# A sample convolution as one product and sum per block, and norm gains applied from PSUM

## The chip, the cores and the metric

The kernel runs on one core of one Trainium2 chip. The metric is the device time of one launch in microseconds (us); lower is better. The time before is the median of three runs.

## What is computed

Two layers (DEPTH = 2) of a decoder for 512 prompt rows (one sequence) and 32 sample rows (8 sequences of 4 new tokens over a paged cache of 2048 positions). Each layer has a mixing part and a gated feed-forward part (FFN):

```python
def hybrid_layer(x, pos, conv_prev, pool_prev, attend, lam_init, p):
    z = rms_norm(x, p['g_mix_pre']) @ p['w_in']              # 1024 -> 2048
    a, ga, u, vb, q, k, v, xd = jnp.split(z, IN_SPLITS, axis=-1)
    ya, conv_new = conformer_conv(a, ga, conv_prev, ...)     # causal depthwise conv, 31 taps, 256 channels
    ...
    mix = jnp.concatenate([ya, yb, yc, yd], axis=-1) @ p['w_out']
    x = x + rms_norm(mix, p['g_mix_post'])
    gate, up = jnp.split(rms_norm(x, p['g_ffn_pre']) @ p['w_gu'], 2, axis=-1)
    x = x + rms_norm((jax.nn.silu(gate) * up) @ p['w_down'], p['g_ffn_post'])
```

The convolution of the sample rows takes 30 earlier rows of state and 4 new ones for each of the 8 sequences: for each of 256 channels (two blocks of 128, the index c) and 32 output tokens, 31 products and their sum. The two places with `rms_norm(...)` behind w_out and w_down are the transitions that the change touches.

## The kernel before, in words

**Numbers.** Weights arrive as fp32 tiles of 128x1024 (`raw`), are cast to a high part `whi` by ScalarE (L194) and a low part `wlo` by VectorE or GpSimd (L197); a product is three matmuls per contraction tile (L130). Activations carry the same two parts, `xhi` and `xlo`.

**Prompt rows.** For a layer the function `mixing` makes the w_in products and the four mixers. Then `prompt` runs `project_last` for w_out: eight (token tile of 128 rows, half of 512 columns) products of 24 matmuls, in the order of W_OUT_TURNS: (0,0) (1,0) (0,1) (1,1) (2,0) (2,1) (3,0) (3,1). Behind each product ScalarE copies the PSUM bank `acc` to `m` (L1282), squares `m` with a running sum (L1286), and GpSimd multiplies `m` by the norm's gain (L1287; VectorE in the last product). When both halves of a tile are there, `finish` makes the factor of the norm (L1297, then `rsqrt`, L177 on VectorE and L178 on GpSimd), the new residual `x_t` (L1305), its squares (L1310), the next norm's rows `m` (L1312), and `turn` (L239 to L242): TensorE transposes `m` into PSUM (`sx`), ScalarE casts that to `xhi`, VectorE subtracts to get `xlo`. Only then can FFN products use the tile. w_down's last chunk goes the same way at the end of the layer, with an add of the PSUM bank to `m` (L1284, VectorE) in place of the copy. At the very end of the kernel the residual of the last tile is made in two halves (L1302).

**Sample rows.** A background generator, `sample`, is interleaved with this. In the mixing part and the transition it runs `sample_pool`, `sample_gate` and `sample_conv`; the latter does the 31 taps by a chain of VectorE instructions of 128x32 (L883), with the buffers of tag "pr" (two of them) for what is loaded and stored (`sst`, `cn`). Behind the convolution come its layer norm, the queries, and the paged attention: per layer 32 gathers of keys (`kr`, L997) and 32 of values (`vr`, L1027) of 512 KB each, issued on GpSimd's queue, four and four for a sequence. Three `kr` and four `vr` buffers are in rotation: a value buffer is free again when TensorE has done the products `sx<-vr` with it.

**Order.** The order of every engine's instructions is fixed when the kernel is built, by a scheduler with its own model of durations; on the chip each engine runs its list in order, waiting on semaphores. So a change of some instructions moves others.

```python
        for t in range(1, CW):
            for c in range(2):
                V.scalar_tensor_tensor(a[:, c], ext[:, c, :, t:t + 4], pf[:, 8 + 2 * t + c:9 + 2 * t + c], a[:, c],
                                       op0=ALU.mult, op1=ALU.add)
...
            if first:
                S.copy(m[t][:, hs], o)
            else:
                V.tensor_tensor(m[t][:, hs], m[t][:, hs], o, op=ALU.add)
...
            (V if (t, half) == (3, 1) else G).tensor_tensor(m[t][:, hs], m[t][:, hs], gain[:, hs], op=ALU.mult)
```

Of the kernel before, what the change touches and what calls it, by code (L numbers as in the profile page):

```python
# [16 lines left out]
DM = 1024  # L17
# [15 lines left out]
# PSUM banks of the two halves of a layer, in address order  # L33
# [3 lines left out]
# priority of the gating chain; buffers of attention weights, and how far scores run ahead of them  # L37
# [3 lines left out]
# input-projection weights whose low part is taken on VectorE  # L41
NV = 1
# convolution taps that ScalarE and GpSimd take
NOFF = 8
# order of w_out's (token tile, half) products, and of its contraction tiles
W_OUT_TURNS = [(0, 0), (1, 0), (0, 1), (1, 1), (2, 0), (2, 1), (3, 0), (3, 1)]
W_OUT_ORDER = (6, 7, 0, 1, 2, 3, 4, 5)
# steps of the sample rows' flow per unit of the prompt's: in the transition, before and while they share weights
# [3 lines left out]
# first FFN feature tile whose weights the sample rows take from the prompt's tiles  # L52
F0 = 10
# buffers of the sample rows' flow; value tiles per round; how far scores run ahead of values
# [10 lines left out]
# columns of the constant block  # L65
C_ID, C_KG, C_BO, C_IW, C_IC, C_QS, C_END = 0, 128, 160, 162, 164, 196, 200
# columns of the sample-attention constant block
# [57 lines left out]
def trunk(ctx, tc, A, O):  # L125
# [18 lines left out]
    def ps():  # L144
        return psx("ps")
# [27 lines left out]
    def rsqrt(pool, src, P, n, scale, eps, tag):  # L173
        """(src * scale + eps) ** -0.5 on a [P, n] block."""
# [47 lines left out]
    def dense_fm(pair, c0, n, tag="acc"):  # L222
        """feature-major product of one weight tile with columns c0..c0+n of the tokens."""
# [9 lines left out]
    def turn(src, P, c0, tag="ps"):  # L233
        """token rows src, transposed into columns c0.. of xhi / xlo."""
# [9 lines left out]
    def finish_sample(fp, parts, m_s, x_t, stage, gpo, gpr, dst, tag):  # L244
        """the sample rows' sublayer output, still in four parts: x_t + its RMS norm, stored; then the RMS norm of that,
        transposed into dst, or xhi / xlo."""
# [90 lines left out]
    # =====================================================================  # L337
    # mixing sub-layer of the prompt (and the input projection of all tokens)
    # =====================================================================
# [12 lines left out]
    def mixing(l, mp, early):  # L352
# [57 lines left out]
        # -- A: convolution  # L410
# [61 lines left out]
        # -- C: attention  # L472
        ST = {}

        def stack():
            for c in range(2):
                st = ST[c] = {}
                # keys out
# [94 lines left out]
        # -- B: spatial gating  # L573
# [52 lines left out]
        # -- D: pooling  # L626
# [226 lines left out]
    def sample_conv(l, mp, cmn):  # L853
# [25 lines left out]
        for c in range(2):  # L879
            V.tensor_scalar(a[:, c], ext[:, c, :, 0:4], pf[:, 8 + c:9 + c], pf[:, c:c + 1], op0=ALU.mult, op1=ALU.add)  # L880
        for t in range(1, CW):
            for c in range(2):
                V.scalar_tensor_tensor(a[:, c], ext[:, c, :, t:t + 4], pf[:, 8 + 2 * t + c:9 + 2 * t + c], a[:, c],  # L883
                                       op0=ALU.mult, op1=ALU.add)
            if t % 4 == 0:
                yield
        o = ps()
# [14 lines left out]

    # =====================================================================
    # sample rows: paged attention, output projection and FFN
    # =====================================================================
    def sample(l, sp, share):
        ys = sp.tile([128, 8, NT], F32, tag="ys", name="ys")
        hs_in = sp.tile([128, 8, NT], F32, name="hs_in")
# [563 lines left out]
```

## Time and profile before

| | |
|---|---|
| time, median of 3 runs | 1460.94 us (1460.93 to 1461.8) |
| span of the profiled execution | 1463.0 us |
| TensorE matmul busy | 1376.9 us, 94% of the span |
| VectorE busy | 832.6 us, 57% |
| ScalarE busy | 499.5 us, 34% |
| GpSimd busy | 451.0 us, 31% |
| chain that ended last | TensorE 72%, VectorE 14%, DMA 5%, GpSimd 3% |

The span is that of one execution taken by the profiler, 2.06 us above the median of the timed runs. PE is TensorE, DVE VectorE, ACT ScalarE, POOL GpSimd, SP SyncE. A busy share is a mean over stages with different limits; the chain says which engine or transfer was waited for, step by step back from the end. The clock column of a table by stretches is the granted TensorE clock as a share of its full speed.

### The profile page before, as it was taken

Reading aid. Unit: us, or ns where it says so; the run is one execution under the profiler, and the core shown is the slowest. Engines: PE = TensorE matmul, PEld = TensorE weight load, DVE = VectorE, ACT = ScalarE, POOL = GpSimd, SP = SyncE. Lnnn points to the kernel's source line nnn. Section 1 sums busy time; section 2 is a strip of 40 time slices with the busy share of each in tenths; the row PEclk is TensorE's granted clock in tenths of the full one; section 3 lists DMA queues with packets and bytes.
Section 4 is the critical chain, followed back from the end, with each engine's and each line's share of the span. In section 5 each row is a group of like instructions: output and inputs, shape, how many; then the busy total and the mean of one; then the engine's idle time right before and its main releaser. Section 6 shows DMA issues by size and latency. Waiting matters only on the chain.

```text
span 1463.0 us, 22985 instructions
## 1 busy us (share of the span) xinstructions
PE 1376.9 (94%) x9114; PEld 1084.0 (74%) x9114; DVE 832.6 (57%) x1536; ACT 499.5 (34%) x987; POOL 451.0 (31%) x415
## 2 busy tenths in 40 slices
PE   6779997999999999999987799989999999999997
PEld 6768876877666777777777788878776667777775
DVE  4986779776434333433659767878664332333344
ACT  4326724332224321222343266333322332222231
POOL 4667545455300000000346685653543000000003
PEclk9989998999999999999998899999999999999999
DMA  6225234888858751233432252466887497213132
GB/s 199 87 69 159 90 120 145 282 317 291 289 169 254 236 180 64 67 107 105 162 105 73 78 149 87 160 217 226 340 302 246 155 309 231 97 58 115 58 133 90
DMA packets 160092, 242.15 MB, mean 166 GB/s; under 512 B 10444, under 2 KB 118226, under 8 KB 159986
## 3 DMA queue, kind: packets, MB, share of 16 engines
q1 hardware_dynamic: 141410, 173.32, 36.9%
q0 software_dynamic: 18432, 67.12, 12.4%
q8 instruction: 72, 1.18, 0.3%
q14 instruction: 34, 0.28, 0.1%
q10 hardware_dynamic: 144, 0.26, 0.0%
HBM read 222.33 MB, written 12.04 MB: 160 GB/s over the span
## 4 chain that ended last, share of the span: by engine, by line
PE 72%; DVE 14%; DMA 5%; issue 3%; POOL 3%; ACT 1%; SPq 0%; DVEq 0%; POOLq 0%; ACTq 0%
PE acc L130 55%; PE sx L130 10%; DVE cacc L422 6%; PE ps L130 3%; DVE sca L883 2%; DMA kr<-in_cache_k_dram,ik 2%; PE s L130 1%; POOL wlo L197 1%; DVE m L1312 1%; PE oT L130 1%; DVE wlo L197 1%; DMA raw<-in_w_in_dram 1%; DMA lq<-in_lambda_k_dram 1%; DVE x_t L1305 1%; PE ps L1012 0%
## 5 line engine op out<-in xcount | busy, mean ns | idle before, releaser
L130 PE MATMUL acc<-xhi,whi 128*128 128x512 f32 (+2 forms) x1152 | 411.6, 358 | 27.1 <-ACT qT L393 15.4
L130 PE MATMUL acc<-xlo,whi 128*128 128x512 f32 (+2 forms) x1152 | 409.0, 355 | 3.4 <-DVE xlo L242 3.4
L130 PE MATMUL acc<-xhi,wlo 128*128 128x512 f32 (+2 forms) x1152 | 409.9, 356 | 0.7 <-POOL wlo L197 0.6
L194 ACT CAST whi<-raw 128x1024 fp32r<-128x1024 f32 x178 | 184.1, 1048 | 298.2 <-PE acc L130 255.9
L130 PEld LDWEIGHTS acc<-xhi,whi 128*128 128x128 f32 x1152 | 223.7, 195 | 67.7 <-ACT qT L393 15.8
L197 DVE TENSOR_TENSOR wlo<-raw,whi 128x1024 fp32r<-128x1024 f32 x144 | 185.6, 1295 | 111.9 <-ACT whi L194 107.7
L130 PEld LDWEIGHTS acc<-xlo,whi 128*128 128x128 f32 x1152 | 224.0, 194 | 34.0 <-issue 4.1
L130 PEld LDWEIGHTS acc<-xhi,wlo 128*128 128x128 f32 x1152 | 224.0, 195 | 32.2 <-issue 4.9
L130 PE MATMUL acc<-whi,h 128*128 128x512 f32 x704 | 226.8, 397 | 0.0
L1287 POOL TENSOR_TENSOR m<-m,g_g_ffn_post 128x512 f32<-128x512 f32 x14 | 19.9, 1423 | 493.0 <-ACT junk L1286 493.0
L130 PEld LDWEIGHTS acc<-whi,h 128*128 128x128 f32 x704 | 131.1, 188 | 44.1 <-issue 11.1
L130 PE MATMUL acc<-wlo,h 128*128 128x512 f32 x352 | 138.6, 395 | 0.0
L422 DVE SCALAR_TENSOR_TENSOR cacc<-hext,pf,cacc 128x512 f32<-128x512 f32 x88 | 115.6, 1336 | 1.9
L197 POOL TENSOR_TENSOR wlo<-raw,whi 128x1024 fp32r<-128x1024 f32 x36 | 96.6, 2691 | 57.1 <-ACT whi L194 57.0
L997 POOL DMA_INDIRECT kr<-in_cache_k_dram,ik x64 | 73.9, 1155 | 106.7 <-DVE kt L1000 73.2
L178 POOL TENSOR_TENSOR rsw<-rsw,mhalf 128x1 f32<-128x1 f32 (+3 forms) x66 | 42.3, 645 | 184.9 <-DVE rsw L177 181.6
L1000 DVE STREAM_TRANSPOSE kt<-kr 128x1024 f32<-128x1024 f32 x64 | 78.3, 1232 | 28.2 <-DMA kr<-in_cache_k_dram,ik 18.5
L1027 POOL DMA_INDIRECT vr<-in_cache_v_dram,iv x64 | 62.8, 981 | 57.0 <-PE sx L130 40.3
L130 PEld LDWEIGHTS acc<-wlo,h 128*128 128x128 f32 x352 | 66.1, 188 | 17.6 <-issue 4.5
L1356 DVE SCALAR_TENSOR_TENSOR th<-th,acc 128x512 f32<-128x512 f32 (+1 forms) x46 | 29.7, 647 | 82.5 <-PE acc L130 82.2
L1165 DVE SCALAR_TENSOR_TENSOR sth<-sth,ps 128x64 f32<-128x64 f32 x22 | 4.8, 220 | 86.4 <-ACT sth L1164 86.4
L130 PE MATMUL sx<-vr,pt 128*32 128x256 f32 x512 | 49.8, 381 | 0.0
(405 smaller groups left out, 1939.6 us busy)
## 6 DMA issues: line engine op xcount, KB each, us to landing
raw<-in_w_gu_dram SPq DMA_DIRECT2D x44, 1024.0 KB
raw<-in_w_down_dram SPq DMA_DIRECT2D x20, 1024.0 KB
rws<-in_w_gu_dram SPq DMA_DIRECT2D x40, 512.0 KB
raw<-in_w_in_dram SPq DMA_DIRECT2D x16, 1024.0 KB
raw<-in_w_out_dram SPq DMA_DIRECT2D x8, 1024.0 KB
rwo<-in_w_out_dram SPq DMA_DIRECT2D x16, 512.0 KB
rws<-in_w_down_dram SPq DMA_DIRECT2D x16, 512.0 KB
x<-x_t SPq DMA_DIRECT2D x12, 512.0 KB
```

The source lines that it names most:

```text
L130: T.matmul(out, lhsT, rhs, start=start, stop=stop)
L178: G.tensor_tensor(y, v, mhalf[:P, :n], op=ALU.pow)
L194: S.copy(hi, src)
L197: eng.tensor_tensor(lo, src, hi.bitcast(F32), op=ALU.subtract)
L422: V.scalar_tensor_tensor(a, hext[c][:, t:t + SEQ], pf[:, 8 + 2 * t + c:9 + 2 * t + c], a, op0=ALU.mult, op1=ALU.add)
L883: V.scalar_tensor_tensor(a[:, c], ext[:, c, :, t:t + 4], pf[:, 8 + 2 * t + c:9 + 2 * t + c], a[:, c], op0=ALU.mult, op1=ALU.add)
L997: G.indirect_dma_start(out=kr, out_offset=None, in_=ck, in_offset=bass.IndirectOffsetOnAxis(ap=ik[:, s, bg:bg + 1], axis=0))
L1000: V.transpose(kt, kr)
L1027: G.indirect_dma_start(out=v.rearrange("p t e -> p (t e)"), out_offset=None, in_=cv, in_offset=bass.IndirectOffsetOnAxis(ap=iv[:, s, a:a + ...
L1287: (V if (t, half) == (3, 1) else G).tensor_tensor(m[t][:, hs], m[t][:, hs], gain[:, hs], op=ALU.mult)
L1305: V.scalar_tensor_tensor(x_t, m[t], r, x_t, op0=ALU.mult, op1=ALU.add)
L1356: V.scalar_tensor_tensor(th[:, :n], th[:, :n], 0.5, ou[:, :n], op0=ALU.mult, op1=ALU.mult)
```

## The change

**Sample convolution.** For each block c of 128 channels and each half of the sequences (hf, four sequences) one VectorE product makes all 31 x 16 = 496 products (tile `sct`, from the "pr" buffers), and one reduction sums them to 16 columns; the bias is added once per block. Per layer that is 4 products, 4 reductions and 2 adds where 2 starts and 60 taps stood.

**Gain, behind w_out.** The copy (L1282) is gone: ScalarE squares straight from the PSUM bank and VectorE multiplies the bank by the gain into `m` (the new L1288).

**Gain, behind w_down.** The multiplication is dropped there; `finish` multiplies by the factor and the gain in one instruction (`m`), and adds that to `x_t` in a second one (L1302 and L1303 of the changed kernel).

GpSimd has no gain instruction any more (28 before). Behind line 880 the changed kernel's line numbers are shifted, by 4 at first and by 12 in `finish`: L1305 is now L1300 (through `add`), L1312 is L1324.

```diff
 a = mp.tile([128, 2, NS, 4], F32, tag="sca", name="sca")
 for c in range(2):
-    V.tensor_scalar(a[:, c], ext[:, c, :, 0:4], pf[:, 8 + c:9 + c], pf[:, c:c + 1], op0=ALU.mult, op1=ALU.add)
-for t in range(1, CW):
-    for c in range(2):
-        V.scalar_tensor_tensor(a[:, c], ext[:, c, :, t:t + 4], pf[:, 8 + 2 * t + c:9 + 2 * t + c], a[:, c],
-                               op0=ALU.mult, op1=ALU.add)
-    if t % 4 == 0:
+    k = pf[:, 8 + c:9 + c]
+    taps_ = bass.AP(k.tensor, k.offset, [k.ap[0], (0, 4), (0, 4), (2, CW)])
+    for hf in range(2):
+        e = ext[:, c, 4 * hf:4 * hf + 4]
+        win = bass.AP(e.tensor, e.offset, [e.ap[0], (34, 4), (1, 4), (1, CW)])
+        pr = cmn.tile([128, 512], F32, tag="pr", bufs=2, name="sct")[:, :16 * CW].rearrange("p (s t j) -> p s t j", s=4, t=4)
+        V.tensor_tensor(pr, win, taps_, op=ALU.mult)
+        V.tensor_reduce(a[:, c, 4 * hf:4 * hf + 4], pr, axis=AX, op=ALU.add)
         yield
+    V.tensor_scalar(a[:, c], a[:, c], pf[:, c:c + 1], None, op0=ALU.add)
...
+junk = jp.tile([128, DM], BF16, tag="ft", bufs=2, name="junk")
 if first:
-    S.copy(m[t][:, hs], o)
+    S.activation(junk[:, hs], o, AF.Square, accum_out=sums[t][:, half:half + 1])
+    V.tensor_tensor(m[t][:, hs], o, gain[:, hs], op=ALU.mult)
 else:
     V.tensor_tensor(m[t][:, hs], m[t][:, hs], o, op=ALU.add)
-junk = jp.tile([128, DM], BF16, tag="ft", bufs=2, name="junk")
-S.activation(junk[:, hs], m[t][:, hs], AF.Square, accum_out=sums[t][:, half:half + 1])
-(V if (t, half) == (3, 1) else G).tensor_tensor(m[t][:, hs], m[t][:, hs], gain[:, hs], op=ALU.mult)
+    S.activation(junk[:, hs], m[t][:, hs], AF.Square, accum_out=sums[t][:, half:half + 1])
...
+def add(hs):
+    if gain is None:
+        V.scalar_tensor_tensor(x_t[:, hs], m[t][:, hs], r, x_t[:, hs], op0=ALU.mult, op1=ALU.add)
+    else:
+        V.scalar_tensor_tensor(m[t][:, hs], m[t][:, hs], r, gain[:, hs], op0=ALU.mult, op1=ALU.mult)
+        V.tensor_tensor(x_t[:, hs], x_t[:, hs], m[t][:, hs], op=ALU.add)
...
-V.scalar_tensor_tensor(x_t, m[t], r, x_t, op0=ALU.mult, op1=ALU.add)
+add(slice(0, DM))
```

The scheduler's order moves with it, at three places.

**Where w_out's second half begins, TensorE, layer 0.** In the kernel before, the transposes of the sample gate (L824) are followed by products of tiles (1,1) and (2,0), which wait for a bank that ScalarE's copy frees:

```order
L824 MATMUL ps_2159<-cst_72,zs_85 32x128 [waits PE_49]
L824 MATMUL ps_2159<-cst_72,zs_85 32x128
L130 MATMUL acc_2338<-whi_2113,yd_1418 128x512 [waits Activation_49]
L130 MATMUL acc_2405<-whi_2093,yd_1418 128x512 [waits Activation_49]
L130 MATMUL acc_2405<-wlo_2094,yd_1418 128x512
L130 MATMUL acc_2405<-whi_2093,yd_1418 128x512 x2
```

This goes on in the same form to its row `acc_2405<-wlo_2094` and further, 21 matmuls in all, before the first product with the second low part of the new weights (`wlo_2114`, made by VectorE). In the changed kernel that product stands right behind the transposes:

```order
L824 MATMUL ps_2158<-cst_72,zs_85 32x128 [waits PE_49]
L824 MATMUL ps_2158<-cst_72,zs_85 32x128
L130 MATMUL acc_2239<-wlo_2114,yd_1418 128x512 [waits DVE_49]
L130 MATMUL acc_2239<-whi_2113,yd_1418 128x512 x2
L130 MATMUL acc_2239<-wlo_2114,yd_1418 128x512
```

Those 21 matmuls now come later, since the bank that they need is freed by VectorE's gain instruction. On VectorE that instruction stands behind the two splits of the same weights:

```order
L866 SCALAR_TENSOR_TENSOR scx_2145<-zs_85 128x8x4 x2
L197 TENSOR_TENSOR wlo_2110<-raw_2107,whi_2109 128x1024 [waits DMAHW3_49,DMAHW7_49,DMAHW0_49,Activation_49]
L197 TENSOR_TENSOR wlo_2114<-raw_2107,whi_2113 128x1024 [waits Activation_49]
L1288 TENSOR_TENSOR m0_2065<-acc_2117,g_g_mix_post_2072 128x512 [waits DMAHW0_49,Activation_49]
L1288 TENSOR_TENSOR m1_2066<-acc_2184,g_g_mix_post_2072 128x512 [waits Activation_49]
```

Before, nothing of the prompt's bank stood there; the copies were on ScalarE.

**The last token tile, VectorE, layer 0.** The kernel before has the last taps ahead of tile 2's norm and nothing of the convolution behind it. In the changed one two of the four products and a reduction stand between tile 3's residual (`x_t_2555`) and its norm (`m3_2068`); the waits DMAHW are for transfers out of or into the "pr" buffers:

```order
L1300 SCALAR_TENSOR_TENSOR x_t_2555<-m3_2068,rsw_2558,x_t_2555 128x1024 [waits DMAHW5_49,DMAHW4_49,Pool_49]
L242 TENSOR_TENSOR xlo_80<-sx_2485,xhi_79 128x4x128 [waits Activation_49]
L887 TENSOR_TENSOR sct_2430<-scx_2145,pf0_82 128x496 [waits DMAHW6_49,DMAHW1_49]
L177 TENSOR_SCALAR rsw_2565<-sumt_2076 128x1 [waits Activation_49]
L888 TENSOR_REDUCE sca_2429<-sct_2430 128x16 [waits DVE_49]
L887 TENSOR_TENSOR sct_2461<-scx_2145,pf0_82 128x496 [waits DMAHW7_49,DMAHW6_49]
L1367 SCALAR_TENSOR_TENSOR th_2711<-th_2711,acc_2661 128x256 [waits Activation_49]
L1324 SCALAR_TENSOR_TENSOR m3_2068<-x_t_2555,rsw_2565,g_g_ffn_pre_2074 128x1024 [waits Pool_49]
```

The rest of the convolution, its layer norm and all that follows it (the queries, the gathers) come behind tile 3's norm.

**Value products, TensorE, layer 0.** Before, the second sequence's value products stand 58 rows behind the last of the first's, with 48 full FFN matmuls of 512 columns between; they begin with these rows, without a break:

```order
L130 MATMUL sx_3283<-kt_3378,qs_2873 32x4x32 [waits DVE_49]
L130 MATMUL sx_3283<-kt_3378,qs_2873 32x4x32 x7
L130 MATMUL sx_3398<-vr_3399,pt_3254 32x256 [waits DMASW1_49,Activation_49]
L130 MATMUL sx_3398<-vr_3401,pt_3254 32x256 [waits DMASW2_49]
L130 MATMUL sx_3398<-vr_3399,pt_3254 32x256
```

In the changed kernel they stand 29 rows behind, with 19 FFN matmuls between, and break up by buffer, with a wait for each:

```order
L130 MATMUL sx_3227<-kt_3266,qs_2761 32x4x32 [waits DVE_49]
L130 MATMUL sx_3227<-kt_3266,qs_2761 32x4x32 x7
L130 MATMUL sx_3342<-vr_3343,pt_3122 32x256 [waits DMASW2_49,Activation_49]
L130 MATMUL sx_3368<-kt_3371,qs_2761 32x4x32 [waits DVE_49]
L130 MATMUL sx_3368<-kt_3371,qs_2761 32x4x32
L130 MATMUL sx_3342<-vr_3345,pt_3122 32x256 [waits DMASW3_49]
L130 MATMUL sx_3342<-vr_3343,pt_3122 32x256
```

The third sequence's stand in the same way behind the second's, with 20 FFN matmuls between, and layer 1 has the like.

## Rows read from the trace of the kernel before

**Rows 1.** Profile page, part 1: busy time, share and instructions by engine.

```profile
PE 1376.9 (94%) x9114; PEld 1084.0 (74%) x9114; DVE 832.6 (57%) x1536; ACT 499.5 (34%) x987; POOL 451.0 (31%) x415
```

**Rows 2.** Stretches: length; busy PE, PEld, DVE, ACT, POOL; granted clock, DMA, GB/s.

```profile
220.00:260.00 40.00, 30.61 (x187) 26.53 (x186) 35.57 (x90) 19.39 (x44) 20.96 (x24) 0.87 0.50 166
300.00:690.00 390.00, 389.85 (x2516) 286.60 (x2515) 163.48 (x260) 106.66 (x174) 49.81 (x49) 1.00 0.56 191
950.00:1000.00 50.00, 44.70 (x344) 41.01 (x343) 38.93 (x112) 19.57 (x43) 21.68 (x24) 0.93 0.60 211
```

**Rows 3.** Timeline, TensorE: start, us, line, tile, count [idle before <- releaser].

```profile
228.15 0.84 PE L239 MATMUL sx<-cst,m 128*128 128x128 f32 x4 [1.59 <-DVE m L1312]
232.24 1.12 PE L239 MATMUL sx<-cst,m 128*128 128x128 f32 x4 [3.25 <-DVE xlo L242]
252.41 1.97 PE L239 MATMUL sx<-cst,m 128*128 128x128 f32 x8 [2.63 <-DVE m L1312]
962.49 0.58 PE L130 MATMUL acc<-xlo,whi 128*128 128x256 f32 x1 [2.10 <-DVE xlo L242]
972.66 1.09 PE L239 MATMUL sx<-cst,m 128*128 128x128 f32 x8 [1.70 <-DVE m L1312]
```

**Rows 4.** Short stretches, TensorE: length, busy us, granted clock, DMA, GB/s.

```profile
232.00:234.00 2.00, 1.76 (x6) 0.50 0.00 0
234.00:236.00 2.00, 2.00 (x8) 0.67 0.00 0
252.00:256.00 4.00, 3.59 (x18) 0.57 0.20 38
964.00:968.00 4.00, 4.00 (x29) 0.78 1.07 353
```

**Rows 5.** Timeline of four engines where w_out's second half begins, layer 0.

```profile
191.73 5.79 POOL L197 TENSOR_TENSOR wlo<-raw,whi 128x1024 fp32r<-128x1024 f32 x2
191.83 6.78 DVE L197 TENSOR_TENSOR wlo<-raw,whi 128x1024 fp32r<-128x1024 f32 x2
194.01 1.07 ACT L1282 COPY m<-acc 128x512 f32<-128x512 f32 x2 [10.77 <-PE acc L130]
194.49 0.38 PE L824 MATMUL ps<-cst,zs 128*32 128x128 f32 x2
199.59 0.39 PE L130 MATMUL acc<-wlo,yc 128*128 128x512 f32 x1
199.82 0.40 PE L130 MATMUL acc<-wlo,yd 128*128 128x512 f32 x1
```

**Rows 6.** Groups on VectorE: line, tile, count | busy us, mean ns | idle.

```profile
L197 DVE TENSOR_TENSOR wlo<-raw,whi 128x1024 fp32r<-128x1024 f32 x144 | 185.6, 1295 | 111.9 <-ACT whi L194 107.7 <-issue 2.4
L883 DVE SCALAR_TENSOR_TENSOR sca<-scx,pf,sca 128x32 f32<-128x32 f32 x120 | 36.0, 357 | 0.0
L1284 DVE TENSOR_TENSOR m<-m,acc 128x512 f32<-128x512 f32 x16 | 10.8, 680 | 16.2 <-PE acc L130 16.2
```

**Rows 7.** Timeline, VectorE and GpSimd, 228 to 232 us.

```profile
228.02 3.57 DVE L883 SCALAR_TENSOR_TENSOR sca<-scx,pf,sca 128x32 f32<-128x32 f32 x2
229.19 2.35 POOL L197 TENSOR_TENSOR wlo<-raw,whi 128x1024 fp32r<-128x1024 f32 x1
```

**Rows 8.** Timeline, gathers on GpSimd and value products on TensorE, layer 0.

```profile
254.66 1.22 POOL L997 DMA_INDIRECT kr<-in_cache_k_dram,ik  x1 [0.19 <-issue]
293.33 2.15 PE L130 MATMUL sx<-vr,pt 128*32 128x256 f32 x26
300.91 0.94 POOL L1027 DMA_INDIRECT vr<-in_cache_v_dram,iv  x1 [0.30 <-issue]
309.60 2.15 PE L130 MATMUL sx<-vr,pt 128*32 128x256 f32 x26
```

**Rows 9.** Timeline, VectorE, end of the kernel.

```profile
1456.64 0.69 DVE L1287 TENSOR_TENSOR m<-m,g_g_ffn_post 128x512 f32<-128x512 f32 x1 [0.85 <-ACT junk L1286]
1458.31 1.41 DVE L1302 SCALAR_TENSOR_TENSOR x_t<-m,rsw,x_t 128x512 f32<-128x512 f32 x2 [0.72 <-POOL rsw L178]
```

More of the change, by code (lines that the diff above doesn't have):

```diff
@@ L1290, in project_last, with finish @@
                 yield from tail(t)
-    def finish(fp, jp, m, sums, t, stage, g, tag="ps"):
+    def finish(fp, jp, m, sums, t, stage, g, tag, gain):
+        def add(hs):
[4 more added lines that the diff above has]
+                V.tensor_tensor(x_t[:, hs], x_t[:, hs], m[t][:, hs], op=ALU.add)
         x_t = fp.tile([128, DM], F32, tag="xio", bufs=2, name="x_t")
@@ L1301, in finish @@
                 hs = slice(512 * i, 512 * i + 512)
-                V.scalar_tensor_tensor(x_t[:, hs], m[t][:, hs], r, x_t[:, hs], op0=ALU.mult, op1=ALU.add)
+                add(hs)
                 eng.dma_start(x_at(stage + 1)(128 * t, 128)[:, hs], x_t[:, hs])
             return
-        V.scalar_tensor_tensor(x_t, m[t], r, x_t, op0=ALU.mult, op1=ALU.add)
+        add(slice(0, DM))
         SY.dma_start(x_at(stage + 1)(128 * t, 128), x_t)
@@ L1325, in prompt @@
                                     gpo, sums, ((None, None), (ring2, ring2)),
-                                    lambda t: finish(tp, fp, m, sums, t, 2 * l, gpr, "sx"),
+                                    lambda t: finish(tp, fp, m, sums, t, 2 * l, gpr, "sx", None),
                                     W_OUT_ORDER, None, PACE_T, W_OUT_TURNS)
@@ L1386, in prompt @@
                 yield from project_last(tp, fp, A["w_down"][l], f0, nf, act, m, False, gpo, sums,
-                                        ((ring2, None), (ring2, ring2)), lambda t: finish(tp, fp, m, sums, t, 2 * l + 1, gpr), None, also)
+                                        ((ring2, None), (ring2, ring2)), lambda t: finish(tp, fp, m, sums, t, 2 * l + 1, gpr, "ps", gpo), None, also)
     def place(stack, name, tags):
```

## The prediction

> **What bounds the kernel now.** I read the page first. TensorE's matmuls are busy for 94% of the span [rows 1], so the other engines matter only where TensorE waits for them. The table by stretches says where that is: in 300 to 690 us TensorE lacks 0.15 of 390 us, while in 220 to 260 us it lacks 9.39 of 40 at a granted clock of 0.87, and in 950 to 1000 us 5.30 of 50 at 0.93 [rows 2]. These two stretches are the w_out transitions of the two layers, and the change works there. The timeline of TensorE names what ends its larger waits: in layer 0, 1.59 us for a norm (L1312), 3.25 us for an `xlo` (L242) and 2.63 us for the last tile's norm; in layer 1, 2.10 and 1.70 us [rows 3]. All five releasers are on VectorE. The clock adds to it: at 232 to 234 us it is 0.50, which is the 1.2 GHz level, and 1.76 busy us do the work of 0.88; the next 2 us at 0.67 lose 0.66, 3.59 us at 0.57 lose 1.54, and in layer 1 4.00 us at 0.78 lose 0.88 [rows 4]. Each of these falls stands close behind waits of [rows 3].
>
> **What the change takes away.** The taps cost 36.0 us of VectorE in both layers, 18.0 in one [rows 6]. The price of the new product and sum has no row; an instruction of 512 columns with a PSUM source, L1284, takes 0.68 us [rows 6], so I take 0.68 as the upper end for each product and each reduction, and 0.36 (a tap, [rows 6]) for each bias add. Four, four and two make at most 6.2 us in place of 18.0. This saves 11.8 us of VectorE in a layer, but only what stands ahead of a waiting TensorE counts. One such place is plain: two taps that together last 3.57 us [rows 7], where the mean for two is 0.71 [rows 6], hold the `xlo` for which TensorE waits 3.25 us. GpSimd runs a weight split meanwhile, 229.19 to 231.54 [rows 7].
>
> For layer 0, of the 1.59 us I count 1.3 gone and of the 3.25 us 2.6 (the subtraction itself must still be made). Of the 2.63 us for the last tile I count 1.5: the copy (1.07 for two, so 0.54 [rows 5]) leaves the chain, and so does the queue of taps, but two products and a reduction come in, ahead of the norm, and the second product waits until a "pr" buffer has been written out. Of the clock's losses I count 0.88 and 0.66 gone, and half of 1.54. That is 5.4 + 2.3 = 7.7 us, between 0 and 10.6 (all of it). For layer 1 in the same way 1.8 of 2.10, 1.2 of 1.70 and the 0.88: 3.9 us, between 0 and 4.7.
>
> **What it adds at the start of the transition.** Before, TensorE ends the gate's transposes at 194.87 (194.49 + 0.38) and goes on with tiles (1,1) and (2,0) until 199.82, when it takes the product with the second low part of VectorE [rows 5]. That could be because ScalarE copied the two banks at 194.01 to 195.08 [rows 5]. Now the bank comes free by the gain on VectorE, behind two splits that begin at 191.83 and end at 198.61 [rows 5]. So TensorE stands from 194.87 to 198.61, **3.74 us** without cover. The 21 matmuls that filled it are not lost but come later. Behind a wait of 3.25 us the clock lost 0.88 + 0.66 us, so I add 1.54: 5.3 us per layer. Layer 1 has the same order; I price it by layer 0's rows. The lower end is 0, if the splits end early (a rival below).
>
> The splits last 3.39 us each where VectorE's mean is 1.29 [rows 5, 6], because GpSimd has two of the same kind from 191.73 to 197.52 [rows 5], where one took 2.35 us in [rows 7]. Taken in turns, 2.35 + 1.29 + 2.35 + 1.29 = 7.28 us would pass; 6.88 did (191.73 to 198.61).
>
> The Trainium skill (SBUF — State Buffer, Who interferes with whom) says that a VectorE instruction with two SBUF inputs and a GpSimd instruction that reads SBUF exclude each other, and that whichever starts first keeps the other out for its whole length. By that rule the trace agrees, and the new gain, with one input in PSUM, would itself not be held: it only stands behind what is.
>
> **The gains, elsewhere.** In the transition a gain on VectorE costs 0.68 (as L1284, [rows 6]), eight per layer; they lie beside TensorE's products, with the exception above. In w_down's transition the gain leaves GpSimd and each tile's residual needs one more pass over 1024 columns on VectorE, which is 2 x 0.68 = 1.36 us ahead of the norm, against a gain that it no longer waits for: 0, within 1.4 either way. At the end of the kernel the last gain (0.69) goes and two halves of 0.7 (1.41 for two) become four [rows 9]: 4 x 0.7 - 1.41 - 0.69 = 0.7 slower, and nothing hides it, since the last store follows.
>
> **What comes later.** The sample rows' gathers begin at 254.66 us [rows 8], behind the convolution, and that now ends behind the last tile's norm. A late start alone would be harmless: the first value products move in the order too. But the second and third sequence's now follow after 19 and 20 FFN matmuls instead of 48. One takes 0.23 us (199.59 to 199.82, [rows 5]), so 29 fewer bring them 6.6 us nearer: before, the rounds are 16.27 us apart (293.33, 309.60), now about 9.7. The last value gather of a round is issued 7.58 us after the round before it (300.91), since it waits for that round's buffers, and has 8.69 us until 309.60 [rows 8]. After the change 2.1 us are left for it. If it needs them all the wait is 6.6 us a round; if it lands within 2.1 us, none. No row says when it lands. Two rounds in two layers: 0 to 26 us. Since TensorE idles only 0.15 us in this stretch before [rows 2], I take little, 0.5 us a round, **2 us** in all; the scheduler breaks the products up by buffer, so the first can run while the last is under way.
>
> **The sum.** Layer 0: -7.7 + 5.3 = -2.4. Layer 1: -3.9 + 5.3 = +1.4. Gathers +2.0, w_down 0, end +0.7. In all **+1.7** on the execution of 1463.0, or 1464.7. The runs' median lies 2.06 below that execution, at 1460.94, so I predict **1462.6**. A measurement of this kernel can tell about 0.2%, or 2.9 us; the forecast is no change.
>
> **Rivals.**
> 1. *Faster: the order of the splits turns.* GpSimd begins its two splits only 0.1 us ahead of VectorE [rows 5]. If VectorE comes first, 1.29 + 2.35 + 1.29 = 4.93 us pass and it ends at 196.76; the wait shrinks from 3.74 to 1.89, and if the clock then holds, 1.85 + 1.54 = 3.4 us are saved per layer: 1462.6 - 6.8 = 1455.8. For it: the margin. Against it: the work ahead of both is unchanged. The Trainium skill (same page and section) states that the order of issue decides who blocks; no run here shows the other order. Chance 0.12.
> 2. *Faster: the transitions empty out.* All the waits of [rows 3] and their clock losses go (another 2.9 + 0.8 us), and the gathers cost nothing (2.0): 1456.9. For it: VectorE's saving of 11.8 us a layer. Against it: tile 3's norm behind a product that waits for a store. Chance 0.16.
> 3. *Slower: value gathers are late.* In each layer two rounds wait for the last value buffer. At 3 us a round (a landing in 5.1 us) it is 12 instead of 2: 1472.6. It decides from a landing of 2.6 us on, where the 0.5 us that I take begin. For it: the buffers rotate once a round, and the distance shrinks by 6.6 us. Against it: the break-up by buffer. Chance 0.22.
> 4. *The taps were not what held VectorE.* GpSimd's weight splits stay, and a norm (L1324) is held by them as a tap was. Then the 2.6 us and 1.54 of clock in layer 0 stay: 1466.7. For it: a split runs right there on GpSimd [rows 7]. Against it: a norm meets a split less often than 60 taps. Chance 0.13.
>
> **Numbers.** My forecast has 0.37. Faster by over 0.2% (below 1458.0): rivals 1 and 2, 0.28. Slower (above 1463.9): rivals 3 and 4, 0.35. Within: 0.37. The likeliest case's own range is 1458 to 1464. The range for 8 in 10 is 1453.5 to 1471: below, both faster rivals in part together; above, rival 3 at a little under 3 us a round.
>
> **What would show it.** Right: TensorE idle for about 3.7 us in front of a product with `wlo` near 195 us and the same in layer 1, with a clock of 0.5 to 0.8 behind it; no `xlo` wait of 3 us later; the last tile's transposes some 2 us earlier in layer 0 and about 1 us later in layer 1; four `sct` products of at most 0.7 us. Wrong: value products with waits of over 1 us each (rival 3), VectorE's splits over before 197 us (rival 1), or a product or reduction of 496 columns much longer than 0.7 us, which would put the last tile later by as much.

## The result: 1.45% slower

The changed kernel takes **1482.81 us** (median of 4 runs, 1481.48 to 1483.5), the kernel before 1461.18 on the same chip: a ratio of 1.0145, 95% interval 1.0133 to 1.0158, or 21.6 us more. The forecast was 1462.6 and the range ended at 1471. The profiled execution spans 1481.3 us against 1463.0, 18.3 more. The two differences need not agree. The profiled execution of the changed kernel has a device time of 1483.04 us, 1.7 more than its span and 0.2 above the median. With the same 1.7, that of the kernel before would have some 1464.7 us (an estimate), which is 3.6 above its median. So the tables by stretches below show some 3 us too little of the loss.

The page of the changed kernel, part 1, and its row for the value products of the sample rows:

```profile
PE 1394.5 (94%) x9114; PEld 1089.9 (74%) x9114; DVE 822.4 (56%) x1453; ACT 492.9 (33%) x971; POOL 405.3 (27%) x387
...
L130 PE MATMUL sx<-vr,pt 128*32 128x256 f32 x512 | 66.1, 382 | 1.1 <-DMA vr<-in_cache_v_dram,iv 1.1
```

The same row of the kernel before:

```profile
L130 PE MATMUL sx<-vr,pt 128*32 128x256 f32 x512 | 49.8, 381 | 0.0
```

TensorE is busy **longer**: 1394.5 us against 1376.9 [rows 1], with the same 9114 matmuls. Nearly all of that stands in one group, 512 value products that took 49.8 us and now take 66.1, at the same mean for one, 382 ns and 381 (the busy time counts matmuls that run at the same time once).

The stretches that answer to [rows 2]; the columns are the same, the second stretch cut in two:

```profile
220.00:260.00 40.00, 36.64 (x234) 32.77 (x233) 29.12 (x49) 15.87 (x35) 9.75 (x12) 0.96 0.31 104
300.00:345.00 45.00, 43.63 (x415) 30.04 (x414) 29.78 (x53) 11.58 (x22) 26.25 (x26) 1.00 0.94 343
345.00:690.00 345.00, 344.73 (x2134) 248.97 (x2133) 135.98 (x216) 93.53 (x153) 29.09 (x29) 1.00 0.52 174
```

The transition of layer 0 is better (36.64 busy where 30.61 stood in [rows 2]); the FFN hardly waits more, 1.37 us and 0.27.

To see where the 18.3 us came in, I cut both traces at the same six places: the first w_out product, the start of the last tile's transposes in w_out's transition (both layers), the start of the sample rows' transposes (`ysm`) in w_down's, the start of the last tile's there, TensorE's last matmul, the end. Each length is a difference of two starts in the timeline.

| stretch, us | before | after | difference | forecast |
|---|---|---|---|---|
| to w_out, layer 0 | 178.5 | 178.9 | +0.4 | 0 |
| w_out's transition, layer 0 | 73.9 | 70.7 | -3.2 | -2.4 |
| FFN, layer 0 | 473.8 | 482.6 | **+8.8** | +1.0 |
| w_down's transition, layer 0 | 29.0 | 31.7 | +2.7 | 0 |
| mixing, layer 1 | 150.1 | 152.3 | +2.2 | 0 |
| w_out's transition, layer 1 | 67.4 | 69.0 | +1.6 | +1.4 |
| FFN and w_down, layer 1 | 482.4 | 487.6 | **+5.2** | +1.0 |
| end, after the last matmul | 7.9 | 8.5 | +0.6 | +0.7 |

The totals of the stretches that I had worked out from rows came nearly as forecast; not all of their terms did, as the section on the prediction says. The timeline of TensorE in the changed kernel, at the places that the prediction named:

```profile
198.94 0.79 PE L130 MATMUL acc<-wlo,yd 128*128 128x512 f32 x1 [3.74 <-DVE wlo L197]
...
249.58 1.97 PE L239 MATMUL sx<-cst,m 128*128 128x128 f32 x8 [3.36 <-DVE m L1324]
...
936.27 0.79 PE L130 MATMUL acc<-wlo,yd 128*128 128x512 f32 x1 [3.75 <-DVE wlo L197]
...
985.16 1.09 PE L239 MATMUL sx<-cst,m 128*128 128x128 f32 x8 [1.73 <-DVE m L1324]
```

The stands in front of the product with `wlo` are there, 3.74 and 3.75 us where 3.74 was forecast; the waits of 1.59, 3.25 and 2.10 us of [rows 3] are gone; the last tile's transposes start 2.83 us earlier than in [rows 3] in layer 0. But the waits in front of these did not shrink: 3.36 us where 2.63 stood, and in layer 1 1.73 where 1.70 stood. The clock behind the stands, in the table of short stretches:

```profile
200.00:204.00 4.00, 4.00 (x11) 0.50 0.10 19
...
936.00:940.00 4.00, 3.73 (x9) 0.50 0.61 204
```

It falls to 0.50, the 1.2 GHz level: 4.00 busy us lose 2.0 and 3.73 lose 1.9, more than the 1.54 that I took from [rows 4]. VectorE's side of it, from its timeline:

```profile
192.18 6.71 DVE L197 TENSOR_TENSOR wlo<-raw,whi 128x1024 fp32r<-128x1024 f32 x2
...
198.81 1.27 DVE L1288 TENSOR_TENSOR m<-acc,g_g_mix_post 128x512 f32<-128x512 f32 x2
...
247.32 0.68 DVE L887 TENSOR_TENSOR sct<-scx,pf 128x496 f32<-128x496 f32 x1 [1.91 <-DMA out_dram<-cn]
...
738.83 3.27 DVE L1303 TENSOR_TENSOR x_t<-x_t,m 128x1024 f32<-128x1024 f32 x1
```

The two splits last 6.71 us and the two gains stand behind them. The second product of the convolution waits 1.91 us for a write-out, ahead of the last tile's norm, as its order said. The last row is one that I had not counted: the new addition to the residual in w_down's transition (L1303) takes 3.27 us, while GpSimd splits a weight from 738.63 to 741.02; the median of the nine such additions is 1.21. By groups on VectorE the new parts cost what was taken for them:

```profile
L1288 DVE TENSOR_TENSOR m<-acc,g_g_mix_post 128x512 f32<-128x512 f32 x16 | 10.8, 683 | 17.9 <-ACT junk L1287 17.9
...
L888 DVE TENSOR_REDUCE sca<-sct 128x16 f32<-128x496 f32 x8 | 5.3, 661 | 0.0
...
L887 DVE TENSOR_TENSOR sct<-scx,pf 128x496 f32<-128x496 f32 x8 | 5.3, 669 | 2.6 <-DMA out_dram<-cn 2.6
```

### The profile page after: what moved, and what is told of

Its sections match the earlier page's. It is cut to its first block, busy times and chain, and to the rows that moved or that the text cites. A ratio compares the mean times of both kernels' runs of the same rounds, so it can differ in the third digit from the quotient of the medians.

```text
span 1481.3 us, 22887 instructions
## 1 busy us (share of the span) xinstructions
PE 1394.5 (94%) x9114; PEld 1089.9 (74%) x9114; DVE 822.4 (56%) x1453; ACT 492.9 (33%) x971; POOL 405.3 (27%) x387
## 4 chain that ended last, share of the span: by engine, by line
PE 73%; DVE 14%; DMA 6%; issue 3%; POOL 2%; ACT 2%; SPq 0%; DVEq 0%; POOLq 0%; ACTq 0%
PE acc L130 56%; PE sx L130 11%; DVE cacc L422 6%; PE ps L130 3%; DVE wlo L197 2%; DMA kr<-in_cache_k_dram,ik 1%; DMA raw<-in_w_gu_dram 1%; PE s L130 1%; ACT whi L194 1%; DMA raw<-in_w_in_dram 1%; DMA out_dram<-cn 1%; PE oT L130 1%; DVE kt L1004 1%; POOL p L528 1%; DMA g_g_mix_pre<-in_g_mix_pre_dram 0%
## 5 line engine op out<-in xcount | busy, mean ns | idle before, releaser
L1001 POOL DMA_INDIRECT kr<-in_cache_k_dram,ik x64 | 70.1, 1095 | 88.2 <-DVE kt L1004 63.8
L1004 DVE STREAM_TRANSPOSE kt<-kr 128x1024 f32<-128x1024 f32 x64 | 78.2, 1231 | 19.7 <-DMA kr<-in_cache_k_dram,ik 13.0
L1031 POOL DMA_INDIRECT vr<-in_cache_v_dram,iv x64 | 62.4, 975 | 79.0 <-PE sx L130 66.6
L130 PEld LDWEIGHTS acc<-wlo,h 128*128 128x128 f32 x352 | 66.1, 188 | 18.0 <-issue 4.8
L130 PE MATMUL sx<-vr,pt 128*32 128x256 f32 x512 | 66.1, 382 | 1.1 <-DMA vr<-in_cache_v_dram,iv 1.1
L130 PEld LDWEIGHTS sx<-vr,pt 128*32 128x32 f32 x512 | 28.4, 109 | 28.2 <-issue 9.8
L429 POOL TENSOR_TENSOR cacc<-cacc,ctap 128x512 f32<-128x512 f32 x28 | 45.5, 1625 | 9.6 <-ACT cacc L427 6.1
```

Source lines behind the costliest of these rows:

```text
L130: T.matmul(out, lhsT, rhs, start=start, stop=stop)
L429: G.tensor_tensor(a2, a2, d, op=ALU.add)
L1001: G.indirect_dma_start(out=kr, out_offset=None, in_=ck, in_offset=bass.IndirectOffsetOnAxis(ap=ik[:, s, bg:bg + 1], axis=0))
L1004: V.transpose(kt, kr)
L1031: G.indirect_dma_start(out=v.rearrange("p t e -> p (t e)"), out_offset=None, in_=cv, in_offset=bass.IndirectOffsetOnAxis(ap=iv[:, s, a:a + ...
```

## Where the loss sits: TensorE's time by kind

The time from one matmul's start to the next one's, less the wait noted between them, summed by kind over the FFN stretches (layer 0 / layer 1, us):

| kernel | stretch | value products | key products | waits |
|---|---|---|---|---|
| before | 473.8 / 482.4 | 22.4 / 22.6 | 18.4 / 18.8 | 0.3 / 1.0 |
| after | 482.6 / 487.6 | 28.8 / 28.5 | 19.7 / 19.9 | 1.6 / 0.4 |

Of the +8.8 in layer 0, 6.4 are value products, 1.3 key products and 1.3 waits; of the +5.2 in layer 1, 5.9 are value products and 1.1 key products, with 0.6 less in waits and 1.1 less in all other matmuls together. The products are the same; what differs is what stands between them. In the timeline of the changed kernel:

```profile
305.11 2.82 PE L130 MATMUL sx<-vr,pt 128*32 128x256 f32 x32
```

```profile
363.67 1.90 PE L130 MATMUL sx<-vr,pt 128*32 128x256 f32 x18
...
367.09 1.91 PE L130 MATMUL sx<-vr,pt 128*32 128x256 f32 x14
```

The first row is a whole round for one sequence (32 matmuls by the trace's count, 2.82 us); the two rows below are another sequence's round in two halves, with six FFN matmuls between, 1.90 + 1.91 = 3.81 us. The granted clock is 1.00 in both places. In the order of layer 0 the value products stand in 24 runs, before in 11. Not every break costs the same, though. If only breaks by full FFN matmuls are counted, the traces show 18 and 17 pieces (layer 0 and 1) where the kernel before has 10 and 10, which is 0.8 us for each piece more in both layers. Breaks by other small matmuls alone cost little: the run with fewer steps below has 20 and 21 runs but 12 pieces a layer, and its value products take 1.9 and 2.4 us more.

## The experiments

Theory after the result: the convolution's code lets the scheduler set the sample rows' work in another order, that order breaks up the value products (and key products), and the broken rounds cost the time. First rival: the gains cause it. Second: the convolution ends late, because its products wait for shared buffers, and lateness is the cause. Each kernel was timed beside the kernel before on the same chip. The kernel before took 1461.2 to 1467.4 us on these occasions (1461.2 and 1466.6 on one and the same chip), so ratios are compared, and "+9.7" is the difference of two medians taken side by side. The times in the expectations are meant for a kernel before of 1461.2. All stretches are compared with the one trace of the kernel before.

### Gains alone

```diff
-            k = pf[:, 8 + c:9 + c]
...
-                V.tensor_tensor(pr, win, taps_, op=ALU.mult)
-                V.tensor_reduce(a[:, c, 4 * hf:4 * hf + 4], pr, axis=AX, op=ALU.add)
+        for t in range(1, CW):
+            for c in range(2):
+                V.scalar_tensor_tensor(a[:, c], ext[:, c, :, t:t + 4], pf[:, 8 + 2 * t + c:9 + 2 * t + c], a[:, c], ...)
+            if t % 4 == 0:
+                yield
```

> The gains as changed, the 60 taps as before. Theory: the loss comes from the sample convolution, which ends late and by that breaks up TensorE's value products in the FFN; the gains cost only the 3.74 us stand at the start of each w_out transition, some 2.7 us in w_down's transition and 0.6 at the end. Then the value products stay in rounds as before (22.4 us of TensorE between the last tile's transposes and w_down, layer 0) and the time is 1464 to 1472. Rival: the gains cause the loss, by the order that PSUM's banks force: 1477 or more, and the value products take 28 us here too.

Measured: ratio 1.0066 (1.0046 to 1.0085), +9.7 us. FFN 474.7 / 482.7, value products 22.7 / 22.8: as before. So the gains don't break them up, as expected, and the difference lies within the 3 to 11 us expected. But part of the cost sits elsewhere than expected: 8.4 us in layer 1's mixing (158.5 for 150.1) and 4.9 in its transition. The timeline shows a wait in the mixing that the kernel before has not:

```profile
906.60 1.97 PE L130 MATMUL oT<-pt,vtok 128*64 128x128 f32 x14 [3.46 <-ACT pt L534]
```

### Convolution alone

```diff
-        for t in range(1, CW):
-            for c in range(2):
-                V.scalar_tensor_tensor(a[:, c], ext[:, c, :, t:t + 4], ...)
...
+                V.tensor_tensor(pr, win, taps_, op=ALU.mult)
+                V.tensor_reduce(a[:, c, 4 * hf:4 * hf + 4], pr, axis=AX, op=ALU.add)
+                yield
```

> The convolution as changed, the gains as before on GpSimd. Theory: the value products are broken up as in the full change and cost 5 to 7 us more per layer, the late gathers 1 or 2; no stand at the start of w_out: 1470 to 1478. Rival (the gains cause the loss): 1456 to 1463.

Measured: 1.0157 (1.0133 to 1.0180), +21.4 us. FFN 490.6 / 493.3, value products 27.5 / 28.2, key products 22.9 / 21.1, waits 5.1 / 3.3. The value products cost 5.1 and 5.5 us more, as expected, but key products and waits add 4.5 and 2.3, and 4.8 and 2.3, which was not expected: the time is above the range of 9 to 17 us. The transitions are short (70.9 and 66.1) and have no stand. So the convolution alone loses as much as the whole change, and its loss falls in the FFN, nearly all of it after the convolution's last instruction of the layer (255.66 us in layer 0). The first rival falls as the cause of the loss in the FFN. The two parts don't add up: 9.7 and 21.4 alone, 21.6 together.

### Its own buffer; sums first

```diff
-            for hf in range(2):
-                e = ext[:, c, 4 * hf:4 * hf + 4]
+            for q in range(8):
+                e = ext[:, c, q:q + 1]
...
-                pr = cmn.tile([128, 512], F32, tag="pr", bufs=2, name="sct")[:, :16 * CW]...
+                pr = mp.tile([128, 4 * CW], F32, tag="sct", bufs=1, name="sct")...
```

> The full change, but the products of the convolution in a buffer of their own, one sequence at a time (16 products and 16 sums of 124 columns per layer in place of 4 and 4 of 496), so that they don't wait for the write-out of the state. Theory that the wait for the buffers makes the convolution late and the lateness breaks the value products: the first gather of layer 0 begins before 258 us, the value products take 23 to 25 us per layer, 1464 to 1472. Rival, that they break up whenever the convolution is short, however early: 27 us or more per layer, 1478 or more.

The other kernel moves the block with the products and sums, unchanged, ahead of the block that writes the state out (`cn`):

```diff
+        a = mp.tile([128, 2, NS, 4], F32, tag="sca", name="sca")
+        for c in range(2):
+            ...
         for hf in range(2):
             o = ps()
...
             SY.dma_start(O[8][l, 4 * hf:4 * hf + 4].rearrange("s t c -> (s t) c"), cn[:120, :256])
             yield
-        a = mp.tile([128, 2, NS, 4], F32, tag="sca", name="sca")
-        for c in range(2):
-            ...
```

> The full change, but the products and sums of the convolution written ahead of the write-out of the state, same size, same buffers. Same question as with the own buffer, by order alone: if lateness is the cause, the first gather of layer 0 begins before 258 us, the value products take 23 to 25 us per layer, and the time is 1464 to 1471; if not, 1478 or more.

Measured: 1.0163 (1.0140 to 1.0186), +22.6 us, and 1.0222 (1.0202 to 1.0242), +34.0 us. The gathers did start early. First GpSimd's timeline of the changed kernel, then with the own buffer:

```profile
262.07 1.23 POOL L1001 DMA_INDIRECT kr<-in_cache_k_dram,ik  x1 [0.19 <-issue]
...
249.79 1.23 POOL L1002 DMA_INDIRECT kr<-in_cache_k_dram,ik  x1 [0.19 <-issue]
```

and at 251.78 with the sums first, where before it was 254.66 [rows 8]. The value products are nearly whole again (23.7 / 23.7 and 23.7 / 24.7), as the theory of lateness had said. But the time came as its rival had said, so lateness falls as the cause of the loss: the gathers are earlier than before, and both kernels are slower than the change. Key products rise to 24.5 / 24.2 and 23.2 / 24.1 and waits to 7.6 / 6.9 and 7.0 / 9.0. Many waits sit inside runs of key products and have no releaser in the profile; with the own buffer, TensorE:

```profile
299.32 0.41 PE L130 MATMUL sx<-kt,qs 128*32 128x128 f32 x4 [0.43 <-issue]
300.06 0.28 PE L130 MATMUL sx<-kt,qs 128*32 128x128 f32 x1 [0.33 <-issue]
300.75 0.40 PE L130 MATMUL sx<-kt,qs 128*32 128x128 f32 x3 [0.41 <-issue]
```

A long run of short products is not enough for such waits: in layer 0 of the kernel before there are three runs of 96 short matmuls (value and key products and transposes) with no full FFN matmul between and no such wait; the run of 84 that is shown here in part has 1.8 us of them. Behind the stretch shown the granted clock is 0.62 from 302.2 to 306.5 us, so these waits cost more than their length.

What stayed was the first theory in a wider form: the order, whatever it breaks.

### The same instructions, three empty steps

The sample rows' flow is a Python generator that is advanced a step at a time among the prompt's work while the kernel is built. The taps had seven steps, the new sum has four. So I gave the steps back and nothing else, behind the sums:

```diff
             V.tensor_scalar(a[:, c], a[:, c], pf[:, c:c + 1], None, op0=ALU.add)
+        for _ in range(3):
+            yield
```

> As the run with the sums ahead of the write-out, plus three empty steps of the sample rows' flow behind the convolution: no instruction is added, only the scheduler is given the rows' later work three steps later (the 60 taps had seven steps, the new sum has four). In its order the value products stand in whole rounds again. Theory that the order, not the convolution's duration, costs the time: between the last tile's transposes and w_down 474 to 477 us in layer 0 (487.5 without the steps) and 482 to 486 in layer 1 (501.6), the ratio to the kernel before 0.998 to 1.006. Rival that the early or late gathers or the convolution itself cost it: 485 or more, ratio 1.012 or more.

> As the run with a buffer of its own, plus the three empty steps. Same question with the other arrangement: by the order theory 474 to 477 us in layer 0 (486.9 without) and 482 to 486 in layer 1 (493.5), ratio 0.998 to 1.006; by the rival no change from 1.016.

The two marks of layer 0's FFN in the timelines, own buffer without and then with the steps:

```profile
246.87 1.09 PE L239 MATMUL sx<-cst,m 128*128 128x128 f32 x8 [0.52 <-DVE m L1325]
...
733.80 0.68 PE L239 MATMUL ps<-cst,ysm 32*128 32x32 f32 x8
```

```profile
246.19 1.09 PE L239 MATMUL sx<-cst,m 128*128 128x128 f32 x8 [0.52 <-DVE m L1327]
...
716.92 0.68 PE L239 MATMUL ps<-cst,ysm 32*128 32x32 f32 x8
```

FFN with the own buffer: 486.9 to **470.7** in layer 0, 493.5 to 479.5 in layer 1; with the sums first: 487.5 to 473.7 and 501.6 to 483.9. Key products are at 18.5 to 18.8 again, value products at 22.7 to 23.3, waits at 0.0 to 1.5. So in these two kernels the loss in the FFN is one of order: not of the convolution's instructions, their length or when the gathers begin (249.12 us with the steps, 249.79 without). The changed kernel itself was not run with three steps more; that its loss has the same cause rests on the run with the convolution alone, on the table by kind and on the run below. As a whole the own buffer with steps takes **0.995** (0.993 to 0.997) of the kernel before, 7.4 us less: faster than both kernels, and better than I had expected (0.998 to 1.006, with an FFN of 474 to 477 and 482 to 486 us). Why its FFN is 3 us shorter than before in each layer is not explained. The sums first with steps stay at 1.0145 (1.0123 to 1.0168), a miss by my numbers: the FFN went as expected, but layer 1's mixing takes 161.9 us there (150.1 before) and its transition 71.3. One wait in that mixing, 3.00 us, stands in front of the same products as that of 3.46 in the run with the gains alone; others, earlier in it, are new (4.86 and 2.95 us).

### Fewer steps in the kernel before

The converse: the old kernel, old taps, with steps taken away.

```diff
-            if t % 4 == 0:
+            if t % 7 == 0:
                 yield
```

> The kernel before, with one number changed: the 60 taps give the scheduler four steps in place of seven (a step behind every seventh tap, not every fourth). Not one instruction is added or taken away. In its order TensorE's value products come in 41 runs instead of 22. Order theory: the stretch between the last tile's transposes and w_down grows from 474 to 480 to 488 us in layer 0 and from 482 to 488 to 496 in layer 1, ratio 1.007 to 1.02. Rival (the breaks are harmless, something in the changed instructions costs the time): ratio within 1.003.

Measured: **1.0209** (1.0192 to 1.0227), +30.8 us, more than the whole change and more than expected. Its marks of layer 0's FFN:

```profile
254.51 1.97 PE L239 MATMUL sx<-cst,m 128*128 128x128 f32 x8 [4.81 <-DVE m L1312]
...
739.97 0.68 PE L239 MATMUL ps<-cst,ysm 32*128 32x32 f32 x8
```

FFN 485.5 / 496.4, that is +11.7 and +14.0, with value products at 24.3 / 25.1, key products at 22.2 / 23.1 and waits at 3.7 / 8.0. The other stretches are within 1.5 us of the kernel before. One number in a Python condition, no instruction changed, and a loss of this kind is there. The rival falls. What it is made of differs: value products are 4.4 us of the 25.7 in the two FFN stretches, key products 8.1 and waits 10.4.

### The stand at the start of w_out, and w_down's gain

```diff
+                src = o
+                if half == 0 and t < 2:
+                    S.copy(m[t][:, hs], o)
+                    src = m[t][:, hs]
-                S.activation(junk[:, hs], o, AF.Square, ...)
-                V.tensor_tensor(m[t][:, hs], o, gain[:, hs], op=ALU.mult)
+                S.activation(junk[:, hs], src, AF.Square, ...)
+                V.tensor_tensor(m[t][:, hs], src, gain[:, hs], op=ALU.mult)
```

> As the run with sums first and empty steps, and in the products (0,0) and (1,0) of w_out ScalarE copies the bank to m again, as before the change (the gain and the squares then read m). Theory: this gives TensorE its cover back, the 3.74 us stand in front of the product with wlo goes in both layers with the slower clock behind it, 4 to 5 us per layer: 7 to 11 us less than without the copies. Rival: the stand only moves behind the 21 matmuls that it had put off, and less than 3 us come of it.

Measured against the sums first with steps: 0.9997 of before (0.9984 to 1.0010), 22.6 us less. But this is no price of the stand. It is gone in both layers; layer 0's transition stays as it was (69.4 to 70.1), layer 1's falls from 71.3 to 63.5, and 9.4 us are the mixing that returns to 152.5. It is far outside the 7 to 11 us expected, since the new order also mended the mixing. A cleaner pair comes below.

```diff
             else:
                 V.tensor_tensor(m[t][:, hs], m[t][:, hs], o, op=ALU.add)
                 S.activation(...)
+                (V if (t, half) == (3, 1) else G).tensor_tensor(m[t][:, hs], m[t][:, hs], gain[:, hs], op=ALU.mult)
...
-    lambda t: finish(tp, fp, m, sums, t, 2 * l + 1, gpr, "ps", gpo)
+    lambda t: finish(tp, fp, m, sums, t, 2 * l + 1, gpr, "ps", None)
```

> As the run before, and w_down's gain back on GpSimd with one residual instruction, as before the change. If the extra pass on VectorE costs what it seemed to in the change's trace (32.5 against 29.0 us between the sample rows' transposes and the last tile's in w_down's transition, 0.6 at the end), 3 to 4 us less than without; if GpSimd's gains hold VectorE as much, within 1.

Measured: 0.9953 (0.9936 to 0.9970), 4.7 us less, as expected or a little more: w_down's transition 32.1 to 29.7, the end 8.5 to 8.0. In these two places the extra pass on VectorE cost 2.9 us (in the change's trace w_down's transition is 2.7 us longer than before, 31.7 for 29.0 and not the 32.5 of the expectation, and the end 0.6). The rest of the 4.7 is not theirs.

> Own buffer and three empty steps (0.995 of before), with w_down's gain back on GpSimd and one residual instruction. From the step measured on the arrangement with the sums first (4.7 us of medians): 0.9915 to 0.9935. If that step was the order's doing there and not the extra pass's: 0.994 to 0.997.

Measured: 0.9966 (0.9954 to 0.9978). The expected gain on top of 0.995 did not come, and the ratio lies where the expectation put the other reading, that the order had done it: w_down's transition is shorter (30.4 to 28.4), but the FFN longer (476.2 / 482.6), with 1.2 / 0.9 us more in key products and 2.3 / 1.4 in waits. The order there is the same in its value products; what else differs is open.

> As the run before, with ScalarE's copy of the bank for the products (0,0) and (1,0) of w_out. The two stands of 3.72 and 3.74 us in front of the product with wlo go. If they are on the path, 3 to 8 us less than without (0.987 to 0.991 of before); if the transition is bound by the last tile's norm anyway, within 2 us of it in layer 0 and some us in layer 1.

Measured: 0.9978 (0.9969 to 0.9988). The stands are gone and the transitions shorten by 2.7 us (66.9 to 64.2) and 1.9 (66.1 to 64.2), a half and a third of the 5.3 that I had priced each at. Layer 1's mixing takes 156.8 instead of 149.7, with the same wait as in the run with the gains alone, so the whole is 1.7 us slower by the medians where 3 to 8 less were expected:

```profile
899.43 1.97 PE L130 MATMUL oT<-pt,vtok 128*64 128x128 f32 x14 [3.46 <-ACT pt L534]
```

### Only w_out's gain

The kernel before with the change of w_out's gain, copies kept for (0,0) and (1,0), and the old taps and w_down.

> The kernel before with w_out's gain applied from PSUM on VectorE (and ScalarE's copy kept for the products (0,0) and (1,0)); the 60 taps and w_down as before. In its order the value products stand as before. What is left of the gains' effect: GpSimd's gain no longer holds VectorE in the transition, 0 to 6 us less than before, ratio 0.996 to 1.000. If the taps still hold the xlo of tile 1, no change (0.998 to 1.002).

Measured: 0.9986 (0.9977 to 0.9995), 2.4 us less. The transitions are 71.5 and 66.6, the FFN 474.8 / 481.7. That is in the expected range: this part of the change, with the copies kept, is a small gain.

## Why the prediction was wrong, point by point

- **The transition of layer 0** (-2.4 forecast, -3.2 measured), **of layer 1** (+1.4 and +1.6) and **the end** (+0.7 and +0.6) came right as totals, and most of their steps did: the `xlo` waits that the taps held went, the stand of 3.74 us came, the second product waited for the write-out. Two terms were wrong and offset each other, so that the totals agree so closely is in part luck. Of the waits for the last tile I counted 1.5 and 1.2 us gone; they are 3.36 for 2.63 and 1.73 for 1.70. And the stand, at 5.3 us in each layer, was priced too high. The prices of 0.68 us for product and sum held (0.669 and 0.661). The clock behind the stand cost more than taken (1.9 to 2.0 us in the worst four, for 1.54); and yet the stand costs less in the end than its length, 2.7 and 1.9 us by the pair of runs. That the last tile's norm also sets the end of the transition would explain it (without the stand TensorE waits 1.67 and 1.02 us for that norm, with it less than 0.7), but this was not tried.
- **The step that failed is "What comes later"**, the term of 2 us for the gathers. I read the new order rightly (rounds broken up, 29 fewer matmuls between) but took it to matter only by a wait for the last buffer, and even counted the break-up in its favour: "the scheduler breaks the products up by buffer, so the first can run while the last is under way". The trace of the change shows the break-up itself as the cost: waits changed by +1.3 and -0.6 us, the value products by +6.4 and +5.9, of +14.0 us in the two FFN stretches; and it stands in the order as built, so no wait for a late gather is needed for it. What makes the scheduler break the rounds up is not shown: with the gathers early the value products were nearly whole again. Rival 3 had the place and nearly the size (12 us), but by the same wrong mechanism.
- **w_down's transition**: 0 forecast within 1.4, +2.7 measured. One of the four new additions runs beside a weight split on GpSimd and takes 3.27 us where 1.21 is usual for it. I had allowed for that with a norm (rival 4) and not with the instruction that the change adds.
- **Mixing in layer 1**: no term forecast, +2.2 measured, up to +11.8 in other orders (161.9). I had not asked whether the order there moves.
- Of the sum, +1.7 forecast and +18.3 in the trace: +12.0 by the gathers' term, +2.7 by w_down, +2.2 by the mixing; the rest is within a microsecond. The medians differ by 21.6; the 3.3 beyond the traces fit the profiled execution of the kernel before, which by the estimate in the section on the result was 3.6 us above its median.

What stays open: why key products cost more and wait without a releaser in some orders (waits of 7 to 9 us in a layer) and not in others. In the change itself this is little (key products +1.3 and +1.1); with the own buffer, the sums first and the fewer steps it is most of the loss in the FFN. It was not tried by itself. Nor was it shown what in the order moves layer 1's mixing.

## What to carry to other kernels

Where a scheduler orders flows that are fed step by step, taking work or steps out of one flow reorders everything behind it: look at how the engine that bounds the kernel finds its instructions afterwards, far from the edit, and count in how many pieces its groups of small products stand, not only waits. When a change to a small part costs time in a place it does not touch, put the flow's number of steps back before judging the part; here that turned 1.016 into 0.995 in one arrangement, and 1.022 into 1.0145 in another, where the new order cost time in the mixing. And when an instruction takes over from another engine, ask which queue its result now stands behind.

## What the runs showed of the hardware that was not expected

- Value products of 32 columns by 128x256 in a whole round of 32 take 2.82 us, and in two halves 3.81, although each has the same mean (381 to 383 ns in every kernel), at a granted clock of 1.00. TensorE's time for them is set here by how many overlap, and a group's mean doesn't show it; its busy sum does (49.8 against 66.1).
- The Trainium skill (SBUF — State Buffer, Who interferes with whom) says that a VectorE instruction with two SBUF inputs contends with a GpSimd instruction that reads SBUF. The trace of the changed kernel agrees: the addition with two SBUF inputs took 3.27 us beside a split, for 1.21. The gain with a PSUM input took a mean of 0.683 us over all 16, but none of them ran beside a split, so whether it would be held is not shown.
